# Splitting four held weight tiles block by block in an mLSTM head's norm, and turning the last head ahead of the way down before it

## The chip, the cores and the metric

One core of a Trainium2 chip runs the whole program. The metric is device time in microseconds, the median of three executions. Five engines work side by side, each in the order in which its instructions were written: TensorE (matmuls; PE in the profile), VectorE (DVE), ScalarE (ACT), GpSimd (POOL) and SyncE (SP), which here only issues DMAs.

## The reference

A trunk of two layers over 512 tokens of 1024 features, all in float32. Each layer is a half-step SwiGLU FFN, a mixer, a second FFN and a gated embedding, each followed by `x <- LayerNorm(alpha * x + sublayer)`. The mixer of layer 0 is an mLSTM, that of layer 1 a gMLP. The change lies in the mLSTM alone:

```
def mlstm_mixer(x, w_in, b_in, conv_w, norm_g, w_out):
    qk, v, z, gates = split(x @ w_in + b_in)
    q, k = split(silu(causal_depthwise_conv(qk, conv_w)))
    h = mlstm_cell(q, k, v, ig, fg)           # 4 heads, 512 values each
    h = (h - mean(h)) * rsqrt(var(h) + eps)   # over each head's 512 values
    h = h * norm_g * sigmoid(z)
    return h @ w_out
```

The cell's `h` is a masked, gated `q k^T` times `v`, over a denominator for each token.

## The kernel before

**Weights.** Every weight tile of 128 x 1024 comes from HBM in float32 (a DMA on SyncE into one of three raw buffers of two tiles each) and is split into an upper part `whi` (ScalarE, L182) and a lower part `wlo` (L183, `raw - whi`, on VectorE, or on GpSimd where the caller passes `low=pool`). A product is then three matmuls (`mm3`): `whi` with the upper part of the data, the other two crosswise. The class `Weights` holds one written order of tiles for the whole program. In the mLSTM six split buffers stand behind it (four "main", two "extra"), so a tile is split when the buffer of the tile six places earlier is released. `release` returns a buffer and splits the next tile at once; `release(later=True)` only notes it in `held`; `refill(n)` returns `n` of the held ones and splits as many tiles.

**The mLSTM, by heads.** For each of four heads, in this order on TensorE: `project_qk` (4 tiles), `project_v` (4), `scores`, `project_z` for parts 0 and 1, `mix`, `project_z` for parts 2 and 3, `down` of the head before (its way down, 4 tiles of `w_out`, added into `xt`), and `gate_turn` of this head. Behind the loop comes the way down of the last head, with the LayerNorm in it. The weight order has the tiles in the same order, so the four tiles held back during `mix` (the buffers of the last two v tiles and the first two z tiles) go to the four tiles of the way down that follows; in head 0, which has none, to the next head's q and k.

**`mix`** multiplies scores by v for token blocks 3, 2, 1, 0 (L933 to L938, two PSUM banks a block: `up` banks for blocks 3 and 2, `dn` banks for 1 and 0) and writes each block's norm behind it: statistics and small steps on VectorE, a power on GpSimd (L952), a small tensor product on VectorE (L953), and the two halves of `hn` (L955, a pair that reads PSUM). TensorE does not wait for these within `mix`. All four splits then follow in `refill(4)`, before the z products' own steps (sigmoid on ScalarE, scaling by `norm_g` on VectorE, L888, and a split on GpSimd with `low=pool`).

**`gate_turn`** transposes `hn` (16 matmuls against the identity, L964, four to a bank, banks `up`, `dn`, `up`, `dn` for blocks 0 to 3), multiplies each block by the z gate on VectorE (L967, `hzf`) and splits it into `hh` and `hl` (L257 on ScalarE, L258 on VectorE), the stationary operands of the way down.

**`down`** runs over four token blocks, two `dn` banks each, and in each over the four tiles, two halves of three matmuls: L252 (`hh`, `whi`), L253 (`hh`, `wlo`), L254 (`hl`, `whi`). A block has 24 matmuls, a way down 96. In the last block each tile is released behind its use. PSUM has four `up` and four `dn` banks, each set used in rotation. At the end of the order the kinds do not follow the cycle of six: the third and fourth tile of the last way down need an "extra" buffer, and get it when the third and fourth tile of the way down before are released.

**Memory.** `near` and `mp` are pools that end with the mLSTM; the next stage's tiles reuse their addresses and wait for the last reader of what lay there. `near` holds tags A (`qh`, then `hn`), B (`ql`, then `sz`), `vh` and `vl`; `hh` and `hl` lie in `mp`. The addresses of `vh` and `vl` become the next stage's small weight buffers (`wquarter`).

Of the kernel before, what the change touches and what calls it, by code (L numbers as in the profile page):

```python
# [10 lines left out]
F32R = mybir.dt.float32r  # L11
# [5 lines left out]
P = 128  # L17
D = 1024
KB = D // P
SEQ = 512  # L20
# [4 lines left out]
HEADS = 4  # L25
# [196 lines left out]
def hybrid_trunk(ctx: ExitStack, tc, x, p, ln_g, ln_b, ffn1_wgu, ffn1_wd, ffn2_wgu, ffn2_wd,  # L222
# [33 lines left out]
    def split(hi, lo, src):  # L256
        sca.activation(hi, src, AF.Copy)  # L257
        vec.tensor_sub(lo, src, hi.bitcast(F32))  # L258

    def up_bank(name):  # L260
        return ps_up.tile([P, 512], F32, name=name, tag="up")
# [4 lines left out]
    def tmp_tile(name):  # L266
        return tmp.tile([P, 512], F32, name=name, tag="tmp")

    def row_ap(src, offset, n):

        return bass.AP(tensor=src.tensor, offset=src.offset + offset, ap=[[0, P], [1, n]])


    W = Weights(nc, raw_pool, split_pool)
# [207 lines left out]
    def col(name, i):  # L482
        c = col_at[name] + i
        return cols[:, c:c + 1]
# [98 lines left out]
    def up(ps, w, t0=0, t1=SEQ, hooked=()):  # L583

        for kb in range(KB):
            if kb in hooked:
                run_hook()
            mm3(ps[:, t0:t1], [a[:, kb] for a in w], xs(kb, t0, t1), kb == 0, kb == KB - 1)
# [147 lines left out]
    def mlstm():  # L736
        b_in = ml_b_in
        with stage_pool("extra", EXTRA) as extra, stage_pool("ml_parts") as near, stage_pool("ml") as mp:
# [83 lines left out]
            def big(tag, dt, name):  # L822
                return (near if tag in "AB" else mp).tile([P, 4, SEQ], dt, name=name, tag=tag)
# [42 lines left out]
            def project_v(h, vb, between=()):  # L866

                ws = []
                vh = near.tile([P, TB, DV + 2], F32R, name="vh", tag="vh")
                vl = near.tile([P, TB, DV], F32R, name="vl", tag="vl")  # L870
                vec.memset(vh[:, :, HV:HV + 2].bitcast(F32), 1.0)
                for t in range(TB):
                    ps = dn_bank("vps")
                    up_tokens(t, ws, ps, release=lambda: None)
                    vf = tmp_tile("vf")
                    vec.tensor_add(vf, ps, vb)
                    split(vh[:, t, :HV], vl[:, t, :HV], vf[:, :HV])
                    split(vh[:, t, HV + 2:], vl[:, t, HV:], vf[:, HV:])
                    if t < len(between) and between[t]:
                        between[t]()  # L880
                return vh, vl

            def project_z(h, sz, i):

                ps = up_bank("zps")
                up(ps, W.take())
                sca.activation(sz[:, i], ps, AF.Sigmoid, bias=col("b_z", h * 4 + i))
                vec.tensor_scalar(sz[:, i], sz[:, i], col("norm_g", h * 4 + i), None, op0=OP.mult)  # L888
                W.release(later=i < 2, low=pool)

            def row_tile():
                return mp.tile([P, SEQ], F32, name="rbc", tag="rbc")

            def load_row(rt, h):
                sca.dma_start(rt, bass.AP(tensor=rows_d.tensor, offset=rows_d.offset + h * SEQ,
                                                ap=[[0, P], [1, SEQ]]))
# [26 lines left out]
            def mix(h, ss, v):  # L923
                vh, vl = v
                hn = big("A", F32, "hn")
                for t in reversed(range(TB)):
                    bank = up_bank if t >= 2 else dn_bank
                    pa, pb = bank("nps"), bank("nps")
                    for j in range(t + 1):
                        s = slice((t - j) * P, (t - j + 1) * P)  # L930
                        sh, sl = ss[j]
                        first, last = j == 0, j == t
                        mm(pa[:, :HV + 2], sh[:, s], vh[:, j, :HV + 2], start=first, stop=False)  # L933
                        mm(pa[:, :HV], sh[:, s], vl[:, j, :HV], start=False, stop=False)
                        mm(pa[:, :HV + 2], sl[:, s], vh[:, j, :HV + 2], start=False, stop=last)
                        mm(pb[:, :HV], sh[:, s], vh[:, j, HV + 2:], start=first, stop=False)
                        mm(pb[:, :HV], sh[:, s], vl[:, j, HV:], start=False, stop=False)
                        mm(pb[:, :HV], sl[:, s], vh[:, j, HV + 2:], start=False, stop=last)  # L938

                    r = small.tile([P, 6], F32, name="hr", tag="hr")  # L940
                    den = pa[:, HV:HV + 1]
                    st = small.tile([P, 2, 6], F32, name="hst", tag="st")
                    vec.bn_stats(st[:, 0], pa[:, :HV])
                    vec.tensor_scalar(r[:, 0:1], den, -1.0, floor[:, t, h:h + 1], op0=OP.mult, op1=OP.max)
                    vec.tensor_max(r[:, 0:1], r[:, 0:1], den)
                    vec.bn_stats(st[:, 1], pb[:, :HV])
                    vec.reciprocal(r[:, 1:2], r[:, 0:1])
                    vec.tensor_mul(r[:, 2:3], r[:, 1:2], r[:, 1:2])
                    mv = small.tile([P, 2], F32, name="hmv", tag="mv")
                    vec.bn_aggr(mv, st)  # L950
                    vec.tensor_scalar(r[:, 3:4], mv[:, 1:2], r[:, 2:3], EPS, op0=OP.mult, op1=OP.add)
                    pool.tensor_tensor(r[:, 4:5], r[:, 3:4], eps_pow, op=OP.pow)  # L952
                    vec.tensor_mul(r[:, 5:6], r[:, 4:5], r[:, 1:2])  # L953
                    for e, ps in enumerate((pa, pb)):
                        vec.tensor_scalar(hn[:, t, e * HV:(e + 1) * HV], ps[:, :HV], mv[:, 0:1], r[:, 5:6],  # L955
                                          op0=OP.subtract, op1=OP.mult)
                return hn

            def gate_turn(h, hn, sz):
                hh, hl = big("hh", F32R, "hh"), big("hl", F32R, "hl")  # L960
                for t in range(TB):
                    ps = (dn_bank if t % 2 else up_bank)("hps").rearrange("p (k c) -> p k c", k=4)
                    for i in range(4):
                        nc.tensor.transpose(ps[:, i], hn[:, t, i * P:(i + 1) * P], ident)  # L964
                    s = slice(t * P, (t + 1) * P)
                    hf = tmp_tile("hzf").rearrange("p (k c) -> p k c", k=4)
                    vec.tensor_mul(hf, ps, sz[:, :, s])  # L967
                    split(hh[:, :, s], hl[:, :, s], hf)
                return [(hh[:, i], hl[:, i]) for i in range(4)]

            prev = None
            for h in range(HEADS):
                vb = mp.tile([P, DV], F32, name="vb", tag="sh0")
                sca.dma_start(vb, row_ap(b_in, 2 * QK + h * DV, DV))
                if h:
                    rt = row_tile()
                    load_row(rt, h)
                qk = project_qk(h)
                if h == 0:
                    rt = row_tile()  # L980
                    v = project_v(h, vb, (None, gate_sums, lambda: (gate_rows(), load_row(rt, h))))
                else:
                    v = project_v(h, vb)
                W.release()
                ss = scores(h, qk, rt)
                sz = big("B", F32, "sz")
                W.release()
                W.release(2, later=True)
                for i in range(2):
                    project_z(h, sz, i)  # L990
                hn = mix(h, ss, v)
                W.refill(4)
                for i in range(2, 4):
                    project_z(h, sz, i)
                if prev is not None:
                    down(prev, h == 1, low=pool)
                else:
                    norm = Norm(0, 1)
                prev = gate_turn(h, hn, sz)
            down(prev, False, norm)  # L1000
            W.close("extra")

# [219 lines left out]
    hooks.extend([lambda: turn_x(2), lambda: turn_x(3), W.fill, load_columns(), load_gates()])  # L1222
    ffn_stage(0, 0)
    mlstm()
    ffn_ple(0, False)
    ffn_stage(1, 0)
# [29 lines left out]
```

## Time and profile before

| | |
|---|---|
| median of three executions | 2293.61 us (2291.57 to 2293.88) |
| the profiled execution, whole | 2293.76 us |
| its span, first to last instruction | 2292.0 us |
| TensorE with a matmul in flight | 2244.7 us, 98% |
| VectorE / ScalarE / GpSimd busy | 1488.8 / 783.8 / 276.6 us |
| mean granted TensorE clock | 0.995 of 2.4 GHz |

The mLSTM lies between about 375 and 802 us. In the rows below, times are microseconds from the span's start, durations too unless said otherwise. `[1.58 <-DVE wlo L183]` means that the engine stood idle 1.58 us before the instruction, ended by that one. A matmul's listed duration includes its way through the array; the next one starts before it ends.

### The profile page before, as it was taken

To read this page: it belongs to the slowest core of one execution; us is meant where nothing else is said; L and a number is where in the kernel's file an instruction comes from. 1 tells how busy PE (TensorE), PEld (TensorE's weight loads), DVE (VectorE), ACT (ScalarE), POOL (GpSimd) and SP (SyncE) were. 2 spreads that over 40 slices of the span, in tenths; PEclk is the share of its full clock that TensorE was granted. 3 is DMA by queue.
4 is the path that set the end of the run, shared out by engine and by line. 5 is a ranking of instruction groups with operands and counts; after the bars stand their busy time and mean duration, and the time that the engine had idled before them with its cause. 6 is when DMAs were issued, how large, how long until landed. Compare 5 with 4: busy or idle time off the path is not lost.

```text
span 2292.0 us, 26053 instructions
## 1 busy us (share of the span) xinstructions
PE 2244.7 (98%) x10622; PEld 1876.8 (82%) x10622; DVE 1488.8 (65%) x2069; ACT 783.8 (34%) x1032; POOL 276.6 (12%) x191
## 2 busy tenths in 40 slices
PE   8999999999999899999999999999999999999997
PEld 7888888887878788888878888887888888888886
DVE  4566658675666655666686566667566674666677
ACT  3333333442524123333343233333233332333332
POOL 1000004122232400000021000002021230000022
PEclk9999999999999999999999999999999999999999
DMA  7322222133231333332332333222322233332212
GB/s 231 107 97 91 92 85 95 55 108 105 69 101 56 120 111 120 105 97 65 111 120 85 113 106 110 92 74 92 129 92 91 75 125 115 129 111 84 82 65 74
DMA packets 172849, 228.30 MB, mean 100 GB/s; under 512 B 4789, under 2 KB 130837, under 8 KB 172729
## 3 DMA queue, kind: packets, MB, share of 16 engines
q1 hardware_dynamic: 165824, 211.83, 28.4%
q10 hardware_dynamic: 6616, 14.69, 1.9%
q8 instruction: 83, 1.36, 0.2%
q14 instruction: 38, 0.30, 0.0%
q0 software_dynamic: 288, 0.12, 0.0%
HBM read 224.51 MB, written 2.11 MB: 99 GB/s over the span
## 4 chain that ended last, share of the span: by engine, by line
issue 47%; PE 25%; DVE 9%; POOL 2%; ACT 1%; POOLq 0%; DVEq 0%; ACTq 0%
PE dps L253 2%; PE dps L254 2%; PE dps L252 2%; DVE xt L521 2%; PE gups L252 1%; PE vps L252 1%; PE gups L253 1%; PE gups L254 1%; PE vps L254 1%; PE vps L253 1%; DVE st L500 1%; PE gvps L253 1%; PE gvps L254 1%; PE gvps L252 1%; PE qps L254 1%
## 5 line engine op out<-in xcount | busy, mean ns | idle before, releaser
L252 PE MATMUL fps<-xh,whi 128*128 128x512 f32 x1312 | 510.6, 389 | 0.0
L253 PE MATMUL fps<-xl,whi 128*128 128x512 f32 x1312 | 510.5, 389 | 0.0
L254 PE MATMUL fps<-xh,wlo 128*128 128x512 f32 x1312 | 510.4, 389 | 0.0
L183 DVE TENSOR_TENSOR wlo<-wraw,whi 128x1024 fp32r<-128x1024 f32 (+1 forms) x274 | 336.0, 1242 | 198.8 <-ACT whi L182 197.1
L182 ACT ACTIVATE whi<-wraw 128x1024 fp32r<-128x1024 f32 (+1 forms) x333 | 343.9, 1048 | 263.6 <-PE dps L254 127.8
L254 PEld LDWEIGHTS fps<-xh,wlo 128*128 128x128 f32 x1312 | 246.3, 188 | 51.4
L252 PEld LDWEIGHTS fps<-xh,whi 128*128 128x128 f32 x1312 | 246.3, 188 | 51.0
L253 PEld LDWEIGHTS fps<-xl,whi 128*128 128x128 f32 x1312 | 246.3, 188 | 50.7
L183 DVE TENSOR_TENSOR wlo<-wquarter,whi 128x1024 fp32r<-128x1024 f32 x112 | 137.3, 1225 | 201.8 <-ACT whi L182 201.8
L182 ACT ACTIVATE whi<-wquarter 128x1024 fp32r<-128x1024 f32 x112 | 118.6, 1059 | 237.7 <-PE gps L254 177.7
L509 POOL TENSOR_TENSOR rs<-rs,eps_pow 128x1 f32<-128x1 f32 x32 | 21.2, 662 | 1470.6 <-DVE rs L508 1470.6
L183 POOL TENSOR_TENSOR wlo<-wraw,whi 128x1024 fp32r<-128x1024 f32 x59 | 151.7, 2577 | 267.8 <-ACT whi L182 236.7
L254 PE MATMUL gps<-whi,flo 128*128 128x512 f32 x448 | 174.3, 389 | 0.0
L252 PE MATMUL gps<-whi,fhi 128*128 128x512 f32 x448 | 174.3, 389 | 0.0
L253 PE MATMUL gps<-wlo,fhi 128*128 128x512 f32 x448 | 174.3, 389 | 0.0
L701 ACT ACTIVATE sg<-fps 128x512 f32<-128x512 f32 x80 | 48.0, 600 | 279.8 <-PE fps L254 279.8
L530 DVE TENSOR_TENSOR xt<-xt,gps 128x512 f32<-128x512 f32 x224 | 143.2, 681 | 0.0
L253 PE MATMUL dps<-wlo,hh 128*128 128x512 f32 x256 | 102.5, 400 | 8.6 <-DVE wlo L183 8.6
L257 ACT ACTIVATE fhi<-h 128x512 fp32r<-128x512 f32 x112 | 69.5, 625 | 116.0 <-DVE h L637 45.9
L252 PE MATMUL dps<-whi,hh 128*128 128x512 f32 x256 | 103.0, 402 | 1.8 <-ACT hh L257 1.8
L254 PE MATMUL dps<-whi,hl 128*128 128x512 f32 x256 | 102.4, 400 | 1.7 <-DVE hl L258 1.7
L258 DVE TENSOR_TENSOR flo<-h,fhi 128x512 fp32r<-128x512 f32 x112 | 75.7, 688 | 36.4 <-ACT fhi L257 36.4
(263 smaller groups left out, 3997.7 us busy)
## 6 DMA issues: line engine op xcount, KB each, us to landing
wraw<-in_ffn_wgu_dram SPq DMA_DIRECT2D x80, 1024.0 KB, 5.4
wquarter<-in_ffn_wd_dram SPq DMA_DIRECT2D x64, 512.0 KB, 3.7
wraw<-in_ml_w_in_dram SPq DMA_DIRECT2D x24, 1024.0 KB, 5.5
wraw<-in_gm_w_in_dram SPq DMA_DIRECT2D x15, 1024.0 KB, 5.8
wraw<-in_ffn_wd_dram SPq DMA_DIRECT2D x12, 1024.0 KB, 4.9
wraw<-in_ml_w_out_dram SPq DMA_DIRECT2D x8, 1024.0 KB, 4.9
wraw<-in_ple_wg_dram SPq DMA_DIRECT2D x8, 1024.0 KB, 5.1
wraw<-in_gm_w_out_dram SPq DMA_DIRECT2D x8, 1024.0 KB, 5.0
```

Of the source, the lines that this page charges most:

```text
L182: self.nc.scalar.activation(hi[:, s], src[:, s], AF.Copy)
L183: (low or self.nc.vector).tensor_sub(lo[:, s], src[:, s], hi[:, s].bitcast(F32))
L252: mm(ps, st[0], mv[0], start=start, stop=False, skip_group_check=more)
L253: mm(ps, st[0], mv[1], start=False, stop=False, skip_group_check=more)
L254: mm(ps, st[1], mv[0], start=False, stop=stop, skip_group_check=more)
L257: sca.activation(hi, src, AF.Copy)
L258: vec.tensor_sub(lo, src, hi.bitcast(F32))
L500: vec.bn_stats(self.st[t][:, i], xt[:, t, i * D // n:(i + 1) * D // n])
L509: pool.tensor_tensor(rs[:, 1:2], rs[:, 0:1], eps_pow, op=OP.pow)
L521: vec.scalar_tensor_tensor(y[:, c], y[:, c], rstd, self.b_bc[:, c], op0=OP.mult, op1=OP.add)
L530: vec.tensor_add(dst, dst, ps)
L701: sca.activation(sg, ps, AF.Silu)
```

## The change

`refill(4)` behind `mix` goes; in its place `refill()`, one tile, stands at the end of each token block's norm. For the last head, `gate_turn` is called before the way down of head 2 instead of behind it, and its `hh` and `hl` take the tags of `vh` and `vl` in `near`, since those of `mp` are still read by that way down. The call of `Norm(0, 1)` in head 0 keeps its place.

```diff
                     for e, ps in enumerate((pa, pb)):
                         vec.tensor_scalar(hn[:, t, e * HV:(e + 1) * HV], ps[:, :HV], mv[:, 0:1], r[:, 5:6],
                                           op0=OP.subtract, op1=OP.mult)
+                    W.refill()
                 return hn
 
             def gate_turn(h, hn, sz):
-                hh, hl = big("hh", F32R, "hh"), big("hl", F32R, "hl")
+                if h < HEADS - 1:
+                    hh, hl = big("hh", F32R, "hh"), big("hl", F32R, "hl")
+                else:
+                    hh, hl = (near.tile([P, 4, SEQ], F32R, name=n, tag=g) for n, g in (("hh", "vh"), ("hl", "vl")))
...
                 hn = mix(h, ss, v)
-                W.refill(4)
                 for i in range(2, 4):
                     project_z(h, sz, i)
+                if h == 0:
+                    norm = Norm(0, 1)
+                last = gate_turn(h, hn, sz) if h == HEADS - 1 else None
                 if prev is not None:
                     down(prev, h == 1, low=pool)
-                else:
-                    norm = Norm(0, 1)
-                prev = gate_turn(h, hn, sz)
+                prev = last or gate_turn(h, hn, sz)
             down(prev, False, norm)
```

## Rows read from the trace of the kernel before

**Rows 1.** The page's first part: busy us, share of the span, instructions.
```profile
PE 2244.7 (98%) x10622; PEld 1876.8 (82%) x10622; DVE 1488.8 (65%) x2069; ACT 783.8 (34%) x1032; POOL 276.6 (12%) x191
```
**Rows 2.** TensorE's waits, 380 to 840: us in total, times, longest.
```profile
PE dps L253 <- DVE wlo L183: 8.6, 6, 1.9
```
**Rows 3.** Timeline of TensorE, head 2's way down: start, us, instruction, idle before.
```profile
640.16 0.39 PE L252 MATMUL dps<-whi,hh 128*128 128x512 f32 x1
642.13 0.50 PE L253 MATMUL dps<-wlo,hh 128*128 128x512 f32 x1 [1.58 <-DVE wlo L183]
...
644.79 0.40 PE L252 MATMUL dps<-whi,hh 128*128 128x512 f32 x1
646.59 0.50 PE L253 MATMUL dps<-wlo,hh 128*128 128x512 f32 x1 [1.40 <-DVE wlo L183]
...
666.06 0.49 PE L964 MATMUL hps<-ident,hn 128*128 128x128 f32 x3
```
**Rows 4.** Timeline of VectorE, head 2's norm and the splits behind it.
```profile
634.10 0.16 DVE L953 TENSOR_TENSOR hr<-hr 128x1 f32<-128x1 f32 x1 [0.66 <-POOL hr L952]
...
637.57 2.35 DVE L953 TENSOR_TENSOR hr<-hr 128x1 f32<-128x1 f32 x1 [0.66 <-POOL hr L952]
...
640.86 6.82 DVE L183 TENSOR_TENSOR wlo<-wraw,whi 128x1024 fp32r<-128x1024 f32 x4
```
**Rows 5.** Timeline of ScalarE, head 2, the upper parts of the four held tiles.
```profile
622.85 3.89 ACT L182 ACTIVATE whi<-wraw 128x1024 fp32r<-128x1024 f32 x4
```
**Rows 6.** Timeline of GpSimd, head 2, the z tiles' subtracts.
```profile
637.50 2.40 POOL L183 TENSOR_TENSOR wlo<-wraw,whi 128x1024 fp32r<-128x1024 f32 x1
642.12 3.34 POOL L183 TENSOR_TENSOR wlo<-wraw,whi 128x1024 fp32r<-128x1024 f32 x1 [2.22 <-ACT whi L182]
```
**Rows 7.** Timeline of TensorE, head 1's way down, its first to behind its last.
```profile
533.83 0.39 PE L252 MATMUL dps<-whi,hh 128*128 128x512 f32 x1
536.09 0.50 PE L253 MATMUL dps<-wlo,hh 128*128 128x512 f32 x1 [1.86 <-DVE wlo L183]
...
539.40 0.80 PE L253 MATMUL dps<-wlo,hh 128*128 128x512 f32 x1 [0.73 <-DVE wlo L183]
...
562.04 0.38 PE L964 MATMUL hps<-ident,hn 128*128 128x128 f32 x2
```
**Rows 8.** Windows: length, PE busy (matmuls), granted clock, DMA share, GB/s.
```profile
533.83:561.90 28.07, 25.48 (x97) 0.88 0.33 113
...
770.05:789.00 18.95, 16.31 (x71) 0.91 0.70 248
```
**Rows 9.** Timeline of TensorE, head 0, its first transposes.
```profile
455.53 0.69 PE L964 MATMUL hps<-ident,hn 128*128 128x128 f32 x3 [0.35 <-DVE hn L955]
```
**Rows 10.** Timeline of VectorE, head 0, the splits and the turn.
```profile
455.75 4.62 DVE L183 TENSOR_TENSOR wlo<-wraw,whi 128x1024 fp32r<-128x1024 f32 x4
...
463.43 0.69 DVE L967 TENSOR_TENSOR hzf<-hps,sz 128x512 f32<-128x512 f32 x1
...
465.43 0.68 DVE L967 TENSOR_TENSOR hzf<-hps,sz 128x512 f32<-128x512 f32 x1
```
**Rows 11.** Timeline of TensorE, head 3's turn and its way down's beginning.
```profile
770.08 1.91 PE L964 MATMUL hps<-ident,hn 128*128 128x128 f32 x16
773.81 0.50 PE L252 MATMUL dps<-whi,hh 128*128 128x512 f32 x1 [1.82 <-ACT hh L257]
...
775.36 0.73 PE L254 MATMUL dps<-whi,hl 128*128 128x512 f32 x1 [0.82 <-DVE hl L258]
```
**Rows 12.** Timeline of GpSimd behind the way down of head 2.
```profile
770.08 10.28 POOL L183 TENSOR_TENSOR wlo<-wraw,whi 128x1024 fp32r<-128x1024 f32 x4 [20.60 <-ACT whi L182]
```
**Rows 13.** Timeline of SyncE's queue near the stage's end.
```profile
780.80 1.49 SPq L154 DMA_DIRECT2D wquarter<-in_ffn_wd_dram  x3
821.20 6.07 SPq L154 DMA_DIRECT2D wraw<-in_ffn_wgu_dram  x3
```
**Rows 14.** Timeline of ScalarE in the next stage: the first split of a small tile.
```profile
867.75 1.05 ACT L182 ACTIVATE whi<-wquarter 128x1024 fp32r<-128x1024 f32 x1
```

## The prediction

> **What bounds it now.** The page's first part comes first: TensorE has a matmul in flight for 98% of the span [rows 1]. The kernel is paced by TensorE's instruction order, and the change adds and removes no matmul, so it can only move the places where TensorE stands still, or runs at its lower clock. TensorE's waits in the mLSTM stretch come next: 8.6 us in six stops on `wlo`, the lower part of a weight split, in `down` [rows 2]. That is two stops in each of heads 1, 2 and 3.
>
> Head 2 shows them. Its way down starts at 640.16 and stands from there to 642.13, and from 644.79 to 646.59. Less one matmul of 0.23 each (the 83 matmuls from 646.59 to 666.06 are 0.234 each) that is 1.74 and 1.57, 3.3 us in all [rows 3]. ScalarE had finished all four upper parts at 626.74 [rows 5]. VectorE wrote the lower parts in one run from 640.86, after the norm's fourth and last block, which is token block 0 [rows 4]. So the cause is VectorE's order: four blocks of 3.47 us (634.10 to 637.57), then the subtracts. The last block is longer: its tensor product on L953 took 2.35 us, where the one before took 0.16, because GpSimd's subtract for the next tile, at 637.50, had started 0.07 us earlier [rows 4, 6].
>
> The rest stands elsewhere. Head 1's way down took 28.2 us (533.83 to 562.04) against head 2's 25.9, with stops that end at 536.09 and 539.40, by the profile 1.86 and 0.73 [rows 3, 7]; head 2's are 1.58 and 1.40 by the same count, so the stops are 0.4 shorter. Its mean granted clock is 0.88: 0.12 x 2 x 28.07 = 6.7 us at 1.2 GHz [rows 8]. They cost 28.2 - 25.9 + 0.4 = 2.7 us. The clock fell right behind the stop of 1.86; the two of head 2 did not bring it down. In front of the last way down, behind the 16 transposes, TensorE stands 1.8 and, two matmuls on, 0.8 us [rows 11], with 0.91 granted over 18.95, so 3.4 us at the low level, which at head 1's 2.7 / 6.7 or somewhat more cost 1.5 us [rows 8].
>
> **The change, part by part.** Times are on head 2's clock; the other heads show the same offsets.
>
> Splitting in the loop puts three lower parts ahead of the norm's last block. One costs 4.62 / 4 = 1.15 us when GpSimd is quiet [rows 10], so block 0 comes 3.5 us later. ScalarE's part is done in time (626.74; the first block's L953 is two periods before 634.10, at 627.2), so nothing waits on data. What queues behind the inserted subtracts on VectorE is the norm of the later blocks, and who waits for that is the transposes and, in the rotation of the four `dn` banks, the way down.
>
> Head 0 has no way down; its transposes follow the z products at once. They started at 455.53, 0.22 before the run of subtracts that follows the last pair, and TensorE already waited 0.35 for that pair [rows 9, 10]. All of 3.5 us shows: **+3.5**.
>
> Heads 1 and 2 lose both stops, -3.3 each, and get one. L953 comes at 637.57 + 3.5 = 641.1. GpSimd's subtract hangs behind its own small power in program order, so it moves along and again starts just before: 641.0 to 643.4. The pair that writes `hn` runs to 644.4. GpSimd's second subtract, which had its data at 642.12, starts at 643.4 and ends at 645.8. The fourth lower part then runs 645.8 to 647.0. TensorE wants it at its 20th matmul, 640.16 + 19 x 0.234 = 644.6. That is a new stop of 2.4 us: **2 x (2.4 - 3.3) = -1.8**. The bounds: if VectorE goes first at 644.4, the stop is 0.9; if it gives way twice, 3.4.
>
> The Trainium skill (SBUF — State Buffer, "Who interferes with whom") says that a VectorE instruction with two SBUF inputs and a GpSimd instruction that reads SBUF exclude each other for the whole instruction, and that the one that issues first has it. The rows on L953 bear this out (2.35 us against 0.16), and by it the stop is 2.4, not 0.9, since GpSimd starts while VectorE is on PSUM inputs.
>
> Head 3's turn now stands ahead of its way down. The transposes can start 0.22 before the run of 640.86, plus 3.5: at 644.1, where the way down began at 640.16, a stop of 4.0. Sixteen take about 1.8 (a row of 1.91) [rows 11]; they were at the end before, so they add nothing. The way down begins at 645.9. VectorE meanwhile writes the fourth lower part to 647.0, scales the last two z tiles (taken as 0.45 each, below a multiply's 0.69), and multiplies the four blocks, one each 2.0 us (463.43 to 465.43) [rows 10]: the fourth ends at 647.9 + 6.0 + 0.7 = 654.6. Turn blocks 1 and 3 hold two of the four `dn` banks, which the way down's second token block needs; it reaches the second of them after 24 + 3 matmuls, at 645.9 + 27 x 0.234 = 652.2. A stop of 2.4, **together 4.0 + 2.4 - 3.3 = +3.1**. What is late next is block 0's residual on VectorE, behind the turn at 656; its banks are wanted at 660, so that is covered.
>
> The last way down follows at once: -1.8 - 0.8, and -1.5 of low clock. It now reaches its fourth tile earlier. That tile's lower part is the second of GpSimd's four, 2.57 each from 770.08, done 5.1 us after the end of the way down before it [rows 12]; it is wanted at 19 x 0.234 = 4.4. **-2.6 + 0.7 - 1.5 = -3.4**.
>
> The new buffers of the last head: the next stage's three small weight loads, issued at 780.80, reuse the address of `vl`, and now wait for the last matmul on `hl` near 800. SyncE's next load stands at 821.20, and the first split of such a tile at 867.75 [rows 13, 14]; with over 60 us of cover this costs nothing. If it were gone, it would be some 20 us of delay for one load. `Norm` for head 0 moves past nothing.
>
> **The clock.** Head 1's low stretch (2.7) goes. New ones: heads 0 and 3 get stops of about 4 us, longer than those that brought it down; I take 2.0 (between 1.5 and 2.7) for head 0, and 0.3 net for head 3, where a slower TensorE uses up the wait on the bank. A stop of 2.4 at heads 1 and 2 is longer than the 1.86 that did it once; as stops of 1.6 didn't, I take 0.6 each, under half a short stretch. 2.0 + 0.3 + 1.2 - 2.7 = **+0.8**. Bounds: -2.7 (no fall) to +6.4 (2.7, 1.0, 2.7, 2.7).
>
> **The sum.** 3.5 - 1.8 + 3.1 - 3.4 + 0.8 = +2.2 us. The profiled execution took 2293.76, 1.8 of it around the span; the median of the runs is 2293.61, so they can be taken as one: **2295.9**. What a measurement here tells from no change is 0.2%, 4.6 us: this is the same.
>
> **The rivals.**
> - The stops change places and nearly cancel (the forecast): 2295.9, chance 0.62, own range 2292 to 2299.
> - Slower by the clock: each long stop brings it down, at heads 1 and 2 too. 2.7 at head 0, 0.3 to 1.0 at head 3, 2.0 to 2.7 at 1 and 2, less 2.7, is 4.3 to 6.4 on the sum of 1.4 without clock: 2299 to 2301. It decides if both heads 1 and 2 fall. For it: both falls followed stops of about 1.8 [rows 7, 8, 11]. Against: four stops of 1.4 to 1.6 didn't. Chance 0.15.
> - Slower by the port: GpSimd's second subtract follows its first with no gap and is ahead of L953 again. Block 0 is 2.4 later at heads 0 and 3, and the stop 1.0 longer at 1 and 2: +6.8, 2302.7. For it: its data is ready. Against: its four at the end take 10.28, not 4 x 2.40, so VectorE does get in between [rows 6, 12]. Chance 0.10.
> - Faster: L953 starts before GpSimd's subtract. Block 0 is 2.4 earlier: head 0 +1.1, heads 1 and 2 a stop of 0.1, so -6.4, head 3 +0.8, the last -3.4, the clock -2: -10, 2283.7. Against: L953 lost by 0.07 us [rows 4, 6], and both follow the same power instruction. Chance 0.08.
> - The splits do not move (buffers or data not free in the loop), only the turn does: head 3 then stops 0.5, 1.1 and 5.4 (bank) for 3.3, the last -3.4: +0.3, 2293.9. ScalarE's early run of four [rows 5] speaks against it: 0.05.
>
> Same is 0.62 + 0.05 less a little at the edge, 0.66; slower 0.26, faster 0.08. The range leaves out the faster rival and the dearer slower one: 2291.6 to 2300.6.
>
> **What would show it.** Right: on VectorE one subtract of 1.2 us behind each `hn` pair, L953 still 2.35 in block 0; TensorE's waits on `hps` of 3.5 to 4 us in heads 0 and 3; one stop on `wlo` of some 2.4 in heads 1 and 2, at the fourth tile; a wait of `dps` on `hzf` in head 3; under 1 us before and in the last way down's first tiles. Wrong: a short L953, or an `hn` pair 2.4 later than said; a fourth lower part before 644.6; a low clock elsewhere.

## The result, and the profile after

Over 20 executions of each the change takes 2295.97 us (2291.61 to 2297.16) and the kernel before 2293.28 us (2289.69 to 2295.52): ratio 1.0013, 95% interval 1.0007 to 1.0019. That is 2.7 us slower, where 2.2 us slower were forecast: inside the 0.2% that the prediction counts as no change, though the interval is clear of 1. The profiled execution is the fastest of the 20, 2291.61 us; a second profile, taken with the first experiment, is of an execution of 2295.38 us, near the median. Both are read here. The second is nearer to the usual case: of the 31 executions of the changed kernel in all, 14 have its mean granted clock of 0.992, 15 have 0.993 or 0.994, and 2, the first profile among them, have 0.995 or more.

TensorE's waits between 380 and 840, first profile of the changed kernel (who waited for whom: us in total, times, longest):

```profile
PE hps L968 <- DVE hn L955: 7.4, 2, 3.7
PE dps L253 <- DVE wlo L183: 4.3, 2, 2.3
PE dps L252 <- DVE hzf L971: 1.9, 1, 1.9
...
PE dps L253 <- POOL wlo L183: 0.3, 1, 0.3
```

The six stops on `wlo` [rows 2] are two, the wait in front of the last way down [rows 11] is gone, and in their place stand two of 3.7 us in front of transposes (0.35 at head 0 before [rows 9]), and one for a PSUM bank. They lie where the forecast put them (timeline of TensorE: start, us, instruction, idle before; head 0, head 1, head 2, head 3, head 3, last way down; `hps` on L968 and `hzf` on L971 are the old L964 and L967):

```profile
458.03 0.87 PE L968 MATMUL hps<-ident,hn 128*128 128x128 f32 x3 [3.68 <-DVE hn L955]
...
545.50 0.50 PE L253 MATMUL dps<-wlo,hh 128*128 128x512 f32 x1 [2.27 <-DVE wlo L183]
...
648.31 0.49 PE L253 MATMUL dps<-wlo,hh 128*128 128x512 f32 x1 [2.01 <-DVE wlo L183]
...
748.33 2.11 PE L968 MATMUL hps<-ident,hn 128*128 128x128 f32 x16 [3.68 <-DVE hn L955]
...
758.58 0.50 PE L252 MATMUL dps<-whi,hh 128*128 128x512 f32 x1 [1.86 <-DVE hzf L971]
...
779.62 0.50 PE L253 MATMUL dps<-wlo,hh 128*128 128x512 f32 x1 [0.26 <-POOL wlo L183]
```

VectorE in head 2, in the same profile, from the third inserted subtract to the fourth:

```profile
639.01 1.22 DVE L183 TENSOR_TENSOR wlo<-wraw,whi 128x1024 fp32r<-128x1024 f32 x1
...
642.51 2.35 DVE L953 TENSOR_TENSOR hr<-hr 128x1 f32<-128x1 f32 x1 [0.66 <-POOL hr L952]
644.90 1.00 DVE L955 TENSOR_SCALAR hn<-nps,hmv,hr 128x256 f32<-128x256 f32 x2
645.82 2.44 DVE L183 TENSOR_TENSOR wlo<-wraw,whi 128x1024 fp32r<-128x1024 f32 x1
```

and GpSimd beside it:

```profile
641.93 0.55 POOL L952 TENSOR_TENSOR hr<-hr,eps_pow 128x1 f32<-128x1 f32 x1 [4.05 <-PE zps L254]
642.44 4.72 POOL L183 TENSOR_TENSOR wlo<-wraw,whi 128x1024 fp32r<-128x1024 f32 x2
```

L953 is held 2.35 us by GpSimd's first subtract, which began 0.07 us earlier, as before [rows 4, 6]. The fourth lower part, 2.44 instead of 1.22, is held by the second, which follows the first without a gap. It is there at 648.26; TensorE wanted it at 646.1 (the way down began at 641.70, 19 matmuls of 0.234 earlier), and that is its stop of 2.01 in head 2.

The stretches of the mLSTM that the change touches, from head 0's third z product to the FFN behind. Columns: length, PE busy (matmuls), granted clock, DMA share, GB/s; the lines are head 0 to its transposes' end, head 1's products up to its norm, the ways down of heads 1 and 2, head 3 from its way down to the first transposes of `xt`, and the whole. The kernel before:

```profile
444.12:457.40 13.28, 12.93 (x67) 1.00 0.09 27
457.40:522.93 65.53, 65.53 (x327) 1.00 0.35 116
533.84:562.04 28.20, 25.61 (x97) 0.88 0.33 112
640.16:666.06 25.90, 22.91 (x97) 1.00 0.37 122
744.18:789.59 45.41, 39.50 (x167) 0.96 0.45 150
444.12:822.56 378.44, 364.68 (x1791) 0.99 0.26 87
```

The changed kernel, first profile (2291.61 us):

```profile
443.29:461.33 18.04, 14.36 (x67) 0.86 0.38 117
461.33:527.73 66.40, 66.40 (x326) 0.99 0.27 88
538.64:563.57 24.93, 22.66 (x97) 1.00 0.24 85
641.70:666.37 24.67, 22.66 (x97) 1.00 0.25 86
744.48:787.90 43.42, 37.62 (x168) 1.00 0.26 81
443.29:820.74 377.45, 361.87 (x1791) 0.99 0.27 87
```

and its second (2295.38 us):

```profile
443.34:461.38 18.04, 14.36 (x66) 0.87 0.35 117
461.38:527.86 66.48, 66.48 (x327) 0.99 0.26 87
538.76:565.09 26.33, 24.05 (x97) 0.94 0.23 80
643.21:669.43 26.22, 24.19 (x97) 0.93 0.23 81
747.53:791.28 43.75, 39.82 (x167) 0.92 0.26 81
443.34:824.13 380.79, 367.03 (x1790) 0.97 0.26 86
```

Head 0 loses 4.8 us and, to a clock that is still low, 0.9 more in the stretch behind it, in both. The two ways down gain 4.5 in the first profile and 1.6 in the second; head 3 with the last way down gains 2.0 and 1.7. Together that is 1.0 us less than the kernel before in the one execution and 2.4 more in the other. What differs between the two is the granted clock, and with it the wait for the bank: 1.00 against 0.94, 0.93 and 0.92 in the ways down, some 14 us more at 1.2 GHz (2 x (0.06 x 26.33 + 0.07 x 26.22 + 0.08 x 43.75)).

### The profile page after: what moved, and what is told of

The parts are those of the page before. It is cut to its first block, busy times and chain, and to the rows that moved or that the text cites. A ratio compares the mean times of both kernels' runs of the same rounds, so it can differ in the third digit from the quotient of the medians.

```text
span 2289.9 us, 26053 instructions
## 1 busy us (share of the span) xinstructions
PE 2241.3 (98%) x10622; PEld 1875.4 (82%) x10622; DVE 1481.6 (65%) x2069; ACT 784.2 (34%) x1032; POOL 269.7 (12%) x191
## 4 chain that ended last, share of the span: by engine, by line
issue 47%; PE 27%; DVE 8%; POOL 2%; ACT 0%; POOLq 0%; ACTq 0%; DVEq 0%
PE dps L253 2%; PE dps L254 2%; PE dps L252 2%; DVE xt L521 2%; PE gups L252 1%; PE vps L252 1%; PE gups L253 1%; PE gups L254 1%; PE vps L253 1%; PE vps L254 1%; PE gvps L253 1%; PE gvps L254 1%; PE gvps L252 1%; DVE st L500 1%; PE zps L252 1%
## 5 line engine op out<-in xcount | busy, mean ns | idle before, releaser
L183 POOL TENSOR_TENSOR wlo<-wraw,whi 128x1024 fp32r<-128x1024 f32 x59 | 145.0, 2470 | 259.2 <-ACT whi L182 195.3
```

The lines of the kernel that those rows point to most:

```text
L183: (low or self.nc.vector).tensor_sub(lo[:, s], src[:, s], hi[:, s].bitcast(F32))
```

## The experiments

Theory: stops change places, at the sizes of the forecast, and the low clock behind the long ones decides about the rest. The rivals are named with each run. Times are medians; the kernel before ran on the same chip in each group (2292.48, then 2292.21, then 2292.09 us). With the changed kernel run again, ten kernels ran.

**The change again.** No edit.

> The changed kernel once more, for a second profile and more times. Theory (stops change places): the same stops to 0.1 us as in the first profile: 3.7 in front of head 0's transposes, 2.3 and 2.0 at the fourth tile of heads 1 and 2, 3.7 and 1.9 in head 3; median 1 to 5 us above the kernel before. What differs between its executions is the low clock: the span differs from the first profile's 2289.9 by about 0.4 us per us of low clock more than 6.8. Rival (the 2.7 us are spread over the program or noise): the stops or the stages outside the mLSTM differ from profile to profile by more than the clock explains.

2295.38 us, ratio 1.0009 (1.0000 to 1.0018). The stops came back to 0.02 us, but for the bank: its wait of 1.9 is missing where the clock is 0.92. There the slower matmuls reach the bank at 762.07, and the turn's last multiply has ended at 761.58. The three stretches with another clock (+1.4, +1.6, +0.3) account for 3.3 of the 3.8 us between the two profiles, and most of the last 0.5 lies behind the mLSTM, so the theory holds in the main. Some 14 us more at the low level cost 3.3 us net, less than the 0.4 for each us that was expected, because the wait on the bank went.

**The splits alone.**

```diff
-                last = gate_turn(h, hn, sz) if h == HEADS - 1 else None
                 if prev is not None:
                     down(prev, h == 1, low=pool)
-                prev = last or gate_turn(h, hn, sz)
+                prev = gate_turn(h, hn, sz)
```

The last head's `hh` and `hl` are in `mp` again, as before.

> The splits in the loop in all four heads, the turn where it was. Theory: +3.3 at head 0, one stop of 2.0 to 2.4 for two of 3.3 together in each of heads 1, 2 and 3 (-1.0 each), the last way down waits 2.6 as before: +0.3 without clock, and with a fall behind head 0's long stop about +2: 2293 to 2297. Rival (splitting is the gain, turning ahead the loss): 2290 or less.

2295.13 us, ratio 1.0010 (1.0001 to 1.0019). Head 0 stands 3.7, heads 1 to 3 once each (6.3 in three), the last way down waits 2.6 as before. Splitting block by block is no gain by itself.

**The turn alone.**

```diff
-                    W.refill()
                 return hn
...
                 hn = mix(h, ss, v)
+                W.refill(4)
```

> The four splits behind the norm as before, the last head's turn ahead of the way down. Theory: heads 0 to 2 as before; head 3 stops 0.5 before its transposes, about 1 at a lower part and about 5 at the bank that the turn holds, for 3.3; the last way down saves 2.6 to 4: within 2 us of the kernel before. Rival (the turn ahead is hidden under the way down): 4 us less than the kernel before.

2291.78 us, ratio 0.9998 (0.9989 to 1.0007). In the place of head 3's stops on `wlo` and of the last way down's wait stand two waits for banks (this kernel's timeline of TensorE):

```profile
757.02 0.80 PE L252 MATMUL dps<-whi,hh 128*128 128x512 f32 x1 [2.91 <-DVE hzf L970]
...
760.99 0.80 PE L252 MATMUL dps<-whi,hh 128*128 128x512 f32 x1 [2.33 <-DVE hzf L970]
```

The columns are those of the timeline above. 5.2 us in all, as expected, but in two pieces, one for each of the turn's two `dn` banks, and without a stop on a lower part. (The profiled execution is the slowest of the eleven, 2295.51 us; its matmuls there are at the low level.) The turn alone is no gain either.

**Head 0 put back.**

```diff
-                    W.refill()
+                    if h:
+                        W.refill()
                 return hn
...
                 hn = mix(h, ss, v)
+                if h == 0:
+                    W.refill(4)
```

> The change, but head 0 splits its four tiles behind the norm, as before. Theory: head 0's stop of 3.7 is back to 0.35 and the low clock behind it does not come: 4 to 6 us less than the change, 2290 to 2292. Rival (head 0's stop is made good by slack later on): as the change, 2296.

2287.69 us, ratio 0.9977 (0.9968 to 0.9986): 7.7 us under the change in the same group, more than the 4 to 6 expected. Head 0's stop is back to 0.33, which with its low clock is the 5.6 of the first two stretches. In this profile, of the fastest of the eleven executions (2285.32 us), the clock did not fall at heads 1 and 2 either, worth 3 us against the second profile of the change; at head 3 it did (0.86 over the 12 us from 740). Whether that comes of the earlier part or is chance, one profile can't tell. The rival (slack later on) is out.

**The z tiles' subtracts on VectorE.**

```diff
-                W.release(later=i < 2, low=pool)
+                W.release(later=i < 2, low=pool if i < 2 else None)
```

> The change, but the subtracts of the last two z tiles' releases run on VectorE, behind the norm, instead of on GpSimd. Theory (GpSimd's subtract, which holds up L953 in block 0 and then the fourth lower part, is 2.2 + 1.2 us of each stop): L953 0.16, head 0's and head 3's first stop 1.5 instead of 3.7, no stop at heads 1 and 2, the wait on the bank in head 3 about 1 longer: 6 to 9 us less than the change, 2286 to 2290. Rival (the order of the norm alone makes the stops, the port adds nothing): within 2 us of the change.

2281.44 us, ratio 0.9951 (0.9938 to 0.9963): 14 us under the change, where 6 to 9 were expected. TensorE's waits in this kernel, between 380 and 840:

```profile
PE hps L968 <- DVE hn L955: 3.1, 2, 1.6
PE dps L252 <- DVE hzf L971: 2.7, 1, 2.7
```

and VectorE's timeline in head 2, block 0:

```profile
636.64 0.16 DVE L953 TENSOR_TENSOR hr<-hr 128x1 f32<-128x1 f32 x1 [0.66 <-POOL hr L952]
636.84 0.99 DVE L955 TENSOR_SCALAR hn<-nps,hmv,hr 128x256 f32<-128x256 f32 x2
637.75 1.22 DVE L183 TENSOR_TENSOR wlo<-wraw,whi 128x1024 fp32r<-128x1024 f32 x1
```

The stops came as expected: 1.5 at heads 0 and 3, none at 1 and 2, the wait for the bank 0.9 longer. What I had left out is the clock: no stretch here is below 1.00, so that the change's some 20 us at the low level (second profile) go too. The same stretches in windows, without head 1's products:

```profile
444.43:458.89 14.46, 12.92 (x66) 1.00 0.37 122
...
535.33:557.72 22.39, 22.39 (x97) 1.00 0.28 94
635.84:658.23 22.39, 22.39 (x98) 1.00 0.29 94
736.34:778.49 42.15, 37.62 (x167) 1.00 0.27 84
444.43:811.33 366.90, 359.01 (x1791) 1.00 0.27 89
```

366.90 against 380.79 in the second profile of the change is 13.9, the whole difference of the medians. A way down without a stop is 22.4 us.

**Two and two.** From the run of the splits alone:

```diff
-                    W.refill()
+                    if h and t >= 2:
+                        W.refill(2)
                 return hn
...
                 hn = mix(h, ss, v)
+                if h == 0:
+                    W.refill(4)
```

> Heads 1 to 3 split two tiles behind block 3 and two behind block 2, none behind blocks 1 and 0; head 0 splits behind the norm and the turn stands behind the way down, both as before. Theory: all four lower parts are there before the way down begins and block 0 comes in time for its banks, so no stop on a weight in heads 1 to 3 (-3.3 each and head 1's low clock), head 0 and the last way down as before: 10 to 13 us under the kernel before, 2280 to 2283. Rival (the norm's blocks, pushed back by 4.6, hold the banks up): a wait of the way down on hn of 1 to 3 us a head, 2285 or more.

2280.62 us, ratio 0.9943 (0.9930 to 0.9955). TensorE's waits between 380 and 840 are four:

```profile
PE dps L252 <- ACT hh L257: 1.8, 1, 1.8
PE sup L253 <- DVE xl L420: 1.5, 1, 1.5
PE dps L254 <- DVE hl L258: 0.8, 1, 0.8
PE hps L966 <- DVE hn L955: 0.3, 1, 0.3
```

No stop on a weight is left in the mLSTM, and no wait on the norm's banks: GpSimd still holds L953 for 2.35, but nobody waits for block 0 then. The last way down waits 2.6, as before.

**The turn inside the way down.** From two and two:

```diff
         for t in range(TB):
+            if inside is not None and t == 2:
+                inside()
             banks = [dn_bank("dps"), dn_bank("dps")]
...
-                    ps = (dn_bank if t % 2 else up_bank)("hps").rearrange("p (k c) -> p k c", k=4)
+                    ps = (dn_bank if t % 2 and h < HEADS - 1 else up_bank)("hps").rearrange("p (k c) -> p k c", k=4)
...
-                    down(prev, h == 1, low=pool)
+                    down(prev, h == 1, low=pool, inside=turn if h == HEADS - 1 else None)
```

with `hh` and `hl` of the last head in `near`, as in the change, and `turn` calling `gate_turn`.

> As the run with two and two, and the last head's turn stands inside the way down, ahead of its third token block, with its transposes in the up banks alone. Theory: the 2.6 us in front of the last way down and the low clock behind them (1.5) go, at most 0.5 comes at its fourth tile: 2 to 4 us less than the run with two and two, 2277 to 2281. Rival (the turn delays the residuals and so the dn banks): nothing gained.

2275.04 us, ratio 0.9924 (0.9911 to 0.9938): 17 us faster than the kernel before, the best of the study. The waits between 380 and 840 are those that the kernel had around the mLSTM anyway, and two of 0.3:

```profile
PE sup L253 <- DVE xl L420: 1.4, 1, 1.4
PE xps L417 <- DVE xt L521: 0.4, 1, 0.4
PE hps L971 <- DVE hn L957: 0.3, 1, 0.3
PE dps L253 <- POOL wlo L183: 0.3, 1, 0.3
```

The whole of the mLSTM's stretch in windows:

```profile
443.45:804.30 360.85, 358.40 (x1790) 1.00 0.28 91
```

Against two and two it is 5.6 us, more than the 2 to 4 expected; 4.8 of it lie in this stretch, which is 365.70 us long there. Low clock behind the wait in front of the last way down was in the expectation, at 1.5 us, but in the profile of two and two it lasted longer: the granted clock is 0.83 over the 20 us from 755, so 6.8 us at the low level, where the kernel before has 3.4 [rows 8].

**The last head's turn in up banks,** in the changed kernel:

```diff
-                    ps = (dn_bank if t % 2 else up_bank)("hps").rearrange("p (k c) -> p k c", k=4)
+                    ps = (dn_bank if t % 2 and h < HEADS - 1 else up_bank)("hps").rearrange("p (k c) -> p k c", k=4)
```

> The change, with the last head's four transposed blocks in up banks instead of up, dn, up, dn. Theory: the wait of the way down on hzf (1.9 where the clock is full) goes, so 0 to 2 us less than the change, 0 in executions whose clock is low there; the 3.7 in front of the transposes stays. Rival (the wait is on VectorE's turn itself, not on the bank): the wait stays 1.9.

2296.29 us, ratio 1.0015 (1.0006 to 1.0024), as the change. Its profile has no wait on `hzf`, but neither has the change's second profile, and the clock was low there in both. It tells nothing about the bank. So the question was asked again where the clock is full, **on the kernel with the z tiles' subtracts on VectorE** (same edit):

> The z tiles' subtracts on VectorE, and the last head's turn in up banks alone: the question of the run in up banks, asked where the clock is full. Theory (the wait of 2.7 on hzf is for the banks that turn blocks 1 and 3 hold): it goes, 2 to 3 us less than with the z subtracts on VectorE alone, 2278 to 2280. Rival (the way down waits for the turn itself, or for the residuals behind it): a wait of 2 us or more stays in the second or third token block, 2281.

2278.80 us, ratio 0.9940 (0.9928 to 0.9953): 2.6 us less than without the edit (in another group; the kernel before took 2292.21 and 2292.09 us in the two), and the wait of 2.7 on `hzf` is gone, with nothing in its place. It was the banks. **And with head 0's splits behind the norm** (the edit of head 0 put back):

> As the run before it, with head 0's four splits behind the norm. Theory: head 0's stop of 1.5 goes back to 0.35 or below, but its norm and turn are as long as before: 1 to 1.5 us less, 2277 to 2279. Rival (the stop at head 0 is hidden): no difference.

2276.27 us, ratio 0.9930 (0.9916 to 0.9943): 2.5 less, where 1 to 1.5 were expected. Head 0's stop went from 1.54 to nothing, below the kernel before, since no subtract of GpSimd holds L953 there; the stretch to the transposes' end is 12.57 us (443.81 to 456.38) against 14.45 (444.06 to 458.51), and the rest of the 2.5 lies outside it.

## Why the prediction was right

**Head 0, +3.5 and 2.0 of clock:** the stop grew from 0.35 to 3.68, and the two stretches by 5.6 with the clock. Right; putting head 0 back shows its weight.

**Heads 1 and 2, two stops for one of 2.4:** stops of 2.27 and 2.01, at the fourth tile, for the reason given: GpSimd's first subtract in front of L953, its second in front of the fourth lower part. Moving these subtracts to VectorE took both stops away. GpSimd, which began first, went first both times, by 0.07 us at L953 (642.44 against 642.51). The Trainium skill (SBUF — State Buffer, "Who interferes with whom") says that of two such instructions the one that issues first blocks the other for its whole length, and these traces agree: 2.35 us with GpSimd's subtract, 0.16 without.

**Head 3, 4.0 and a bank's 2.4:** 3.68 and 1.86, and up banks remove the second. Right in mechanism, the two together 0.9 shorter than forecast; the second is there only where the clock stays full.

**The last way down, -3.4:** the gain is too small. Head 3 and the last way down together were to come out even (3.1 - 3.4 + 0.3) and gained 2.0 and 1.7. The stop that it kept is 0.26, not 0.7: beside residuals and statistics, which read PSUM or one SBUF operand, GpSimd's subtracts are not slowed as they were beside the turn [rows 12]; the four take 9.46 now (GpSimd's timeline, first profile):

```profile
774.82 9.46 POOL L183 TENSOR_TENSOR wlo<-wraw,whi 128x1024 fp32r<-128x1024 f32 x4 [24.93 <-ACT whi L182]
```

And the waits removed were taken from the idle column, 2.6, where start to start they are 3.0: 773.81 less the 16 transposes' 1.75 from 770.08 is 2.0, and the second one 1.0.

**The clock, +0.8:** right in sign, and it is the term that varies. The first profile has one fall, at head 0; the second has falls at heads 0 to 3, where 0.6 each were put down for heads 1 and 2. The two ways down gained 1.6 there, where 3.3 were forecast with the clock, so 1.7 is missing; head 3 and the last way down gained 1.7 beyond their forecast of nothing. So the closeness of 2295.9 to 2295.97 is in part luck: two errors that offset each other.

The cover for the small weight loads held: they were issued at 799.96 instead of 780.80, right behind the last way down, and the next load followed at 819.38 in its old place.

The rivals: L953 was not let ahead (faster), GpSimd's second subtract did not get ahead of it either (slower by the port), the splits did move. The condition of the clock rival, a fall at both heads 1 and 2, held in the second profile. 14 of the 31 executions have that profile's mean clock; if the clock fell at the same places in them, which no other profile of this kernel shows, a chance of 0.15 was too low. But it came to +2.4 for the stretch, not to +5.7 or more: the falls at heads 1 and 2 cost 1.4 and 1.6, not 2.0 to 2.7 each, and head 3 with the last way down gained 1.7 all the same, since the bank's wait went. Why the clock falls at a stop in one execution and not in the next stays open.

## What to carry to other kernels

Work that is moved up in an engine's queue moves everything behind it down: look up who waits for each step that is pushed back. Put the moved work ahead of steps that nobody waits for soon (here all four tiles behind the first two blocks, in the heads with a way down between norm and transposes), or leave it where it was (head 0, whose transposes follow at once). A transposed operand that takes banks out of another product's rotation was no cheaper ahead of that product; in its middle, in other banks, it left no wait above 0.3 us. And when stops of 2 us or more are traded for longer ones, take several profiles, since the clock behind them differs from execution to execution.

## What the runs showed of the hardware

The same stop need not bring the clock down. In front of head 3's transposes TensorE stood 3.68 us in one execution and 3.67 in another; the granted clock over the 43 us from there on was 1.00 in the first and 0.92 in the second. At heads 1 and 2, behind stops of 2.0 to 2.3, it was 1.00 and 0.93 to 0.94. Of the 3.8 us between the two executions, 3.3 lie in these stretches.

A two-operand instruction of VectorE on a column of 128 x 1 took 0.16 us alone and 2.35 us when GpSimd's 128 x 1024 subtract had begun 0.07 us before it; with GpSimd's two subtracts per head moved to VectorE, which does them in 1.22 us each, the kernel was 14 us faster.
